# Output projection summed operand by operand, first queries asked for earlier, the gate's norm weight as a per-partition scale, and table loads moved, in a decoder block on one core

## The chip, the cores and the metric

The kernel runs on one core of a Trainium2 chip. The metric is device time in microseconds for one execution of the whole block; the median of the runs is taken. Engines are named as the profile names them: PE (TensorE, matmuls) and PEld (its weight loads), DVE (VectorE), ACT (ScalarE), POOL (GpSimd) and SP (SyncE). Here POOL and SP mainly issue transfers.

## What is computed

One decoder block over 2048 tokens of width 1024, all in float32. The input is normalised and modulated, projected once, and split between four heads of gated linear attention (GLA) and eight heads of dilated softmax attention. Their outputs are put side by side and pass through one output projection. Then follows a gated feed-forward layer with a causal convolution.

```python
h = rms_norm(x, norm1_g[l]) * (1 + sc1) + sh1
proj = h @ w_in[l]
gq, gk, gv, gr, glr, aq, ak, av = jnp.split(proj, split_at, axis=-1)
...
# gla_group, at its end
o = rms_norm(o, norm_g).reshape(B, S, H * GLA_DV)
return (o * jax.nn.silu(r.astype(jnp.float32))).astype(r.dtype)
...
mixed = jnp.concatenate([y_gla.astype(x.dtype), y_att.reshape(B, S, ATTN_DIM).astype(x.dtype)], axis=-1)
x = x + g1 * (mixed @ w_out[l])

h = rms_norm(x, norm2_g[l]) * (1 + sc2) + sh2
u = causal_depthwise_conv(h @ w_up[l], conv_w[l], conv_b[l])
u_gate, u_val = jnp.split(u, 2, axis=-1)
x = x + g2 * ((jax.nn.silu(u_gate) * u_val) @ w_down[l])
```

## The kernel before

**Tiles and products.** The sequence is cut into four chunks of T = 512 tokens. Activations lie with features on the 128 partitions, so a chunk of width 1024 is KD = 8 tiles of 128x512. Each float32 product is made of three matmuls (`mm3`, lines 317 to 319): operand and weight are each split in a high part and a remainder, and high x high, low x high, high x low are summed in a PSUM bank. For an operand the high part is a cast (ACT), the remainder a subtraction (DVE). The names are hhi and hlo, or ghi and glo, by the pool that the tiles come from; whi and wlo for weights.

**Weights.** `plan` lists the weight blocks in the order of use. `wslot` loads a block of 512 KB into one of two wraw buffers (POOL, L246), casts it to whi (ACT, L251) and subtracts for wlo (DVE, L252); whi and wlo have four buffers each. A block's request needs a free wraw buffer, and its cast a free whi buffer.

**Two streams.** Generators are woven into each other: the stream of large products (projection `proj` of all chunks, then for each chunk the output projection `outproj` and the feed-forward layer `ffn`), and beside it the mixing of each chunk, `mix(c)`: `gla` for the two halves a = 0, 1 of the chunk, then `attn` for four pairs of heads. A scheduler, given the program in this order, then orders the instructions of each engine by a timeline of its own. Each engine works its list strictly in order. The output projection of chunk 0 follows the projection of chunk 3, and runs beside the first steps of `gla(1, 0)`.

**PSUM.** Eight banks of 128x512: four (psg) for the large products, four (psa) for mixing and statistics.

**Output projection.** For each of eight column blocks cb it takes a bank and a weight block, sums over all eight operands, and adds the scaled bank to x1 (DVE, L1163). The eight operands are the mixing's outputs y, reloaded from DRAM (POOL, L1087) and split (ACT L1088, DVE L1089); the last one is still on the chip. For chunk 0 the operands are placed in pools that are free then: the first five in gp, the sixth in up, the last two in hp. The other chunks take all from hp.

**Mixing.** `gla` sums the log decays (PE L694, copied by DVE L695), forms decay factors relative to several positions (DVE L732, L735, L736 and ACT L733, L734) and multiplies them (PE L712). At its end come a Square with sums (ACT L796), a Sqrt (ACT L799), a scaling (DVE L805), transposes (PE L811), evacuations into buffers with the tag stage (two of them, shared with other users) and stores of y (SP, L814). `attn_first` loads keys kt and queries qf of a pair of heads; for later pairs it is called one pair ahead. PE L930 multiplies them. The wide projection column `wide(1)` makes the gate rg: Tanh (ACT L580), two operations of DVE (L582, and L583 with the norm weight), store.

**Norms.** For the queries and keys of attention the squares are split (ACT L520, DVE L521) and summed by PE (L526, L527); the inverse root comes from a logarithm and an exponential (ACT L528, L529), then DVE L424 to L426 and L532. The chunk's input norm does the same (PE L455, L456; ACT L461, L462), followed by DVE L479 and L483. ACT keeps one set of function tables at a time; the program holds an ACT_TABLE_LOAD wherever another is needed.

## Time and profile before

| what | us |
|---|---|
| median of 3 runs | 2571.36 |
| lowest and highest | 2571.28, 2572.19 |
| profiled execution | 2572.54 |
| its span, first to last instruction | 2570.7 |
| PE busy in it | 2536.8 (99%) |
| DVE, ACT, POOL busy | 1908.6 (74%), 1270.1 (49%), 446.9 (17%) |
| mean granted clock of PE | 0.997 of full |

Busy time is the union of an engine's instructions, so a PE that is busy may still be slow: at half clock its matmuls take longer and stay "busy". The wait of an instruction is the idle time of its engine just before it, with the instruction or transfer that ended last named behind an arrow.

### The profile page before, as it was taken

How to read it: one execution, taken by the hardware profiler on the slowest of the kernel's cores; microseconds unless marked ns; L12 is line 12 of the kernel's file. 1: busy time of each engine (PE TensorE's matmuls, PEld its weight loads, DVE VectorE, ACT ScalarE, POOL GpSimd, SP SyncE). 2: the span in 40 equal slices, each digit the busy share in tenths (PEclk: the TensorE clock that was granted, in tenths of full speed). 3: DMA queues.
4: the chain of work that ended last, by engine and by line, in shares of the span. 5: the costliest groups of instructions: out<-in, count | busy, mean ns of one | idle time of the engine just before them, and what ended most of it. 6: DMA issues, size and time to landing. Idle time of an engine off the chain costs nothing.

```text
span 2570.7 us, 49713 instructions
## 1 busy us (share of the span) xinstructions
PE 2536.8 (99%) x19458; PEld 2092.3 (81%) x19458; DVE 1908.6 (74%) x4135; ACT 1270.1 (49%) x2624; POOL 446.9 (17%) x814
## 2 busy tenths in 40 slices
PE   7999999999999999999999999999999999999999
PEld 4888788888788888888888888888888888888887
DVE  7678877767778677777977777778777776766665
ACT  5556756655554444454545444445445443433332
POOL 2333332322310000112100000310000003200001
PEclk9999999999999999999999999999999999999999
DMA  8775675665733344446434444743444536433332
GB/s 328 265 239 188 201 251 163 222 214 162 238 120 91 115 138 141 129 158 200 140 97 131 141 141 143 232 141 107 122 141 143 149 103 209 141 97 99 98 99 82
DMA packets 189727, 406.38 MB, mean 158 GB/s; under 512 B 48515, under 2 KB 89525, under 8 KB 188213
## 3 DMA queue, kind: packets, MB, share of 16 engines
q0 software_dynamic: 88096, 308.59, 36.9%
q1 hardware_dynamic: 101396, 94.60, 12.5%
q8 instruction: 154, 2.52, 0.4%
q14 instruction: 81, 0.66, 0.1%
HBM read 341.25 MB, written 61.87 MB: 157 GB/s over the span
## 4 chain that ended last, share of the span: by engine, by line
PE 93%; DVE 2%; DMA 2%; issue 1%; ACT 1%; POOL 0%; POOLq 0%; DVEq 0%; ACTq 0%
PE psg L317 27%; PE psg L318 27%; PE psg L319 27%; PE psa L907 2%; PE psa L879 2%; PE psa L1034 2%; PE psa L712 2%; PE psa L930 1%; PE psa L1028 1%; PE psa L785 0%; PE psa L784 0%; PE psa L459 0%; PE psa L789 0%; PE psg L1212 0%; DMA y<-stage 0%
## 5 line engine op out<-in xcount | busy, mean ns | idle before, releaser
L317 PE MATMUL psg<-hhi,whi 128*128 128x512 f32 x1968 | 773.0, 394 | 0.3 <-DVE x L1163 0.3
L318 PE MATMUL psg<-hlo,whi 128*128 128x512 f32 x1968 | 770.3, 392 | 0.0
L319 PE MATMUL psg<-hhi,wlo 128*128 128x512 f32 x1968 | 770.0, 391 | 0.0
L251 ACT CAST whi<-wraw 128x1024 fp32r<-128x1024 f32 (+1 forms) x388 | 407.0, 1049 | 455.6 <-PE psg L318 392.0
L252 DVE TENSOR_TENSOR wlo<-wraw,whi 128x1024 fp32r<-128x1024 f32 (+1 forms) x388 | 474.7, 1224 | 205.7 <-ACT whi L251 198.1
L317 PEld LDWEIGHTS psg<-hhi,whi 128*128 128x128 f32 x1968 | 369.9, 188 | 78.1 <-issue 0.6
L319 PEld LDWEIGHTS psg<-hhi,wlo 128*128 128x128 f32 x1968 | 369.9, 188 | 77.2 <-issue 0.3
L318 PEld LDWEIGHTS psg<-hlo,whi 128*128 128x128 f32 x1968 | 369.9, 188 | 75.9 <-issue 0.7
L317 PE MATMUL psg<-ghi,whi 128*128 128x512 f32 x744 | 296.9, 400 | 0.3 <-DVE x L1163 0.3
L318 PE MATMUL psg<-glo,whi 128*128 128x512 f32 x744 | 293.4, 394 | 1.6 <-DVE glo L1089 1.6
L319 PE MATMUL psg<-ghi,wlo 128*128 128x512 f32 x744 | 293.0, 394 | 0.0
L246 POOL DMA_DIRECT2D wraw<-in_w_up_dram x176 | 96.8, 550 | 975.8 <-DVE wlo L252 764.1
L1163 DVE SCALAR_TENSOR_TENSOR x<-psg,mod,x 128x512 f32<-128x512 f32 x192 | 143.1, 748 | 116.2 <-PE psg L319 115.8
L317 PE MATMUL psg<-whi,hhi 128*128 128x512 f32 (+2 forms) x512 | 173.8, 344 | 2.2 <-ACT stg L585 1.5
L318 PE MATMUL psg<-wlo,hhi 128*128 128x512 f32 (+2 forms) x512 | 174.4, 342 | 0.0
L319 PE MATMUL psg<-whi,hlo 128*128 128x512 f32 (+2 forms) x512 | 173.2, 341 | 0.0
L317 PEld LDWEIGHTS psg<-ghi,whi 128*128 128x128 f32 x744 | 140.5, 189 | 31.5 <-issue 0.9
L318 PEld LDWEIGHTS psg<-glo,whi 128*128 128x128 f32 x744 | 140.4, 189 | 30.7 <-DVE glo L1089 2.3
L319 PEld LDWEIGHTS psg<-ghi,wlo 128*128 128x128 f32 x744 | 140.3, 189 | 29.6 <-issue 0.2
L1118 ACT ACTIVATE y<-psg,tables_sb 128x512 f32<-128x512 f32 x176 | 135.8, 772 | 5.4 <-PE psg L319 4.8
L1119 DVE SCALAR_TENSOR_TENSOR y<-psg,tables_sb,y 128x511 f32<-128x511 f32 x176 | 130.8, 743 | 3.5 <-ACT y L1118 3.4
L1120 DVE SCALAR_TENSOR_TENSOR y<-psg,tables_sb,y 128x510 f32<-128x510 f32 x176 | 130.6, 743 | 0.5
(279 smaller groups left out, 3610.5 us busy)
## 6 DMA issues: line engine op xcount, KB each, us to landing
wraw<-in_w_up_dram POOLq DMA_DIRECT2D x176, 512.0 KB, 3.8
wraw<-in_w_down_dram POOLq DMA_DIRECT2D x88, 512.0 KB, 3.8
wraw<-in_w_ch_dram POOLq DMA_DIRECT2D x44, 512.0 KB, 4.5
wada<-in_w_ada_dram POOLq DMA_DIRECT2D x64, 256.0 KB, 4.8
wraw<-in_w_tokw_dram POOLq DMA_DIRECT2D x32, 512.0 KB, 4.6
wraw<-in_w_out_dram POOLq DMA_DIRECT2D x32, 512.0 KB, 4.5
sq<-in_xT_dram POOLq DMA_DIRECT2D x48, 256.0 KB, 5.0
x<-x POOLq DMA_DIRECT2D x48, 256.0 KB, 5.4
```

The costliest lines, as they stand in the source:

```text
L246: ld = self.dq.dma_start(raw[:, :n], src)
L251: nc.scalar.copy(hi[:, :n], raw[:, :n])
L252: nc.vector.tensor_tensor(lo[:, :n], raw[:, :n], hi[:, :n].bitcast(F32), op=ALU.subtract)
L317: nc.tensor.matmul(ps, wh, hh, start=first and k == 0, stop=False, skip_group_check=shared)
L318: nc.tensor.matmul(ps, wh, hl, start=False, stop=False, skip_group_check=shared)
L319: self.lastmm = nc.tensor.matmul(ps, wl, hh, start=False, stop=k == n - 1, skip_group_check=shared)
L712: nc.tensor.matmul(sp[j:j + w, o + n * w:o + (n + 1) * w], kh[R, k0:k0 + w], qh[R, q0:q0 + w], start=True, stop=True)
L879: nc.tensor.matmul(at(i, hh, o, n)[H[z]], q(H[hh], i, z), key(H[hh], i, k0, n), start=True, stop=True, skip_group_check=True)
L1118: nc.scalar.activation(y, ps, AF.Identity, bias=self.cb[:, b:b + 1], scale=self.cw[:, 2, b:b + 1])
L1119: nc.vector.scalar_tensor_tensor(y[:, 1:], ps[:, :T - 1], self.cw[:, 1, b:b + 1], y[:, 1:], op0=ALU.mult, op1=ALU.add)
L1120: nc.vector.scalar_tensor_tensor(y[:, 2:], ps[:, :T - 2], self.cw[:, 0, b:b + 1], y[:, 2:], op0=ALU.mult, op1=ALU.add)
L1163: nc.vector.scalar_tensor_tensor(x1, ps, self.mod[:, 40 + cb:41 + cb], x1, op0=ALU.mult, op1=ALU.add)
```

## The change

Four edits.

1. The output projection's first four blocks take four banks at once and are summed operand by operand: a new arrangement of the weights, w_outk, holds in slot j the rows of operands 2j and 2j+1 for the four blocks' 512 columns. Blocks 4 to 7 stay as they were. For chunk 0 the operands are placed anew: the first two in hp, the next five in gp, the last in up.
2. `attn_first(c, 0)` is called at the end of `gla(c, 1)`, ahead of its transposes and stores, and the queries' buffer comes from the tag pt (five buffers) instead of stage (two).
3. The gate's multiplication by the norm weight (L583) and the load of that weight are gone. The weight, a column more in the tables, times 0.5, scales the evacuation of the transposed outputs, where it is one number per partition.
4. The table set that holds logarithm and exponential is asked for after the last Tanh of `wide(1)`, and for chunk 0 after the Sqrt of `gla`, instead of at the decay's first product. The program has 29 table loads instead of 36.

```diff
@@ plan
-            yield from (("w_out", (b,), KD, P) for b in range(KD))
+            yield from (("w_outk", (j,), 2, T) for j in range(4))
+            yield from (("w_out", (b,), KD, P) for b in range(4))
@@ consts, ada_setup
-        self.gB = self.cload("gla_norm_g", (P, P))
...
+        nc.vector.tensor_scalar(self.gy, gy, 0.5, None, op0=ALU.mult)
...
+    def logexp(self, last):
+        pre = self.nc.scalar.preload_act_table_set("natural_log_exp_and_others")
+        self.tc.add_manual_dep(pre.ins, last.ins.name, mybir.DependencyInfo(mybir.DependencyClass.Sync, mybir.DependencyReason.DATA))
@@ proj, wide(1)
-                    nc.scalar.activation(st, pss[s], AF.Tanh, scale=0.5)
+                    tanh = nc.scalar.activation(st, pss[s], AF.Tanh, scale=0.5)
+                    if s == 3 and not put_off:
+                        self.logexp(tanh)
                     nc.scalar.copy(r, pss[s])
                     nc.vector.scalar_tensor_tensor(st, st, 1.0, r, op0=ALU.add, op1=ALU.mult)
-                    heads = lambda t: t.rearrange("p (a n) -> p a n", a=4)
-                    nc.vector.scalar_tensor_tensor(heads(st), heads(st), 0.5, self.gB[:, None, :].to_broadcast([P, 4, P]), op0=ALU.mult, op1=ALU.mult)
@@ the decay
-            if a == 0:
-                self.tie(nc.scalar.preload_act_table_set("natural_log_exp_and_others"), mm)
@@ gla
-        nc.scalar.activation(ss, ss, AF.Sqrt, bias=self.eps, scale=1.0 / P)
+        root = nc.scalar.activation(ss, ss, AF.Sqrt, bias=self.eps, scale=1.0 / P)
+        if c == 0:
+            self.logexp(root)
...
+        if a:
+            ready.append(self.attn_first(c, 0))
         yield
...
             st = t2("stage", 2)
-            self.copy(st, ps)
+            if s:
+                nc.scalar.activation(st, ps, AF.Copy, scale=self.gy)
+            else:
+                nc.vector.tensor_scalar(st, ps, self.gy, None, op0=ALU.mult)
@@ attn_first, attn, mix
-        qf = self.at.tile([P, T], F32, name="qf", tag="stage", bufs=2)
+        qf = self.at.tile([P, T], F32, name="qf", tag="pt", bufs=5)
...
-        kt, qf = ready.pop() if ready else self.attn_first(c, hp)
+        kt, qf = ready.pop()
@@ outproj
-            if c or k > 5:
+            if c or k < 2:
                 hi, lo = (self.hp.tile([P, T], F32R, name=n) for n in ("hhi", "hlo"))
-            elif k == 5:
+            elif k == KD - 1:
                 hi, lo = (self.up.tile([P, T], F32R, name=n, tag=n) for n in ("y0", "y1"))
...
-        for cb in range(KD):
+        def leave(cb, ps):
+            nc.vector.scalar_tensor_tensor(x1[cb], ps, self.mod[:, 16 + cb:17 + cb], x1[cb], op0=ALU.mult, op1=ALU.add)
+
+        pss = [self.pg() for _ in range(4)]
+        for j in range(4):
+            w = self.weights("w_outk", j)
+            order = [(i, cb) for i in range(2) for cb in range(4)]
+            if j == 3:
+                order.sort(key=lambda x: x[1])
+            for i, cb in order:
+                n = slice(cb * P, (cb + 1) * P)
+                self.mm3(pss[cb], [(w[i][0][:, n], w[i][1][:, n])], hs[2 * j + i:2 * j + i + 1], i == 0 and j == 0, True)
+            if j < 3:
+                yield
+        for cb in range(4):
+            leave(cb, pss[cb])
+        yield
+        for cb in range(4, KD):
             ps = self.pg()
-            self.mm3(ps, self.weights("w_out", cb), hs)
-            nc.vector.scalar_tensor_tensor(x1[cb], ps, self.mod[:, 16 + cb:17 + cb], x1[cb], op0=ALU.mult, op1=ALU.add)
+            self.mm3(ps, self.weights("w_out", cb - 4), hs)
+            leave(cb, ps)
             yield
@@ layout (host)
-        ... gla_norm_g=np.broadcast_to(gla_norm_g.reshape(1, P), (P, P)),
-        w_out=pack_blocks(w_out[0], P), ...
+        w_outk=wide(w_out[0][:, 0:512]), w_out=pack_blocks(w_out[0][:, 512:], P), ...
```

Lines below 413 keep their numbers but for one or two; later ones move on: L526 and L527 are L530 and L531 in the changed kernel, L712 is L713, L736 is L737, L796 and L799 are L797 and L800, L930 is L938, L1088 and L1089 are L1096 and L1097, L1163 of the output projection is L1102.

The scheduler's lists show the edits where they move other work. First PE, from the end of chunk 3's projection (psg_7350 is its last bank) into the output projection of chunk 0, before; psg_7495, psg_7534 and psg_7643 are the banks of blocks 0, 1 and 2, and numbers in names tell buffers apart:

```order
3010 L319 MATMUL psg_7350<-hhi_5750,wlo_7167 128x512
3011 L526 MATMUL psa_7326<-sqr_7319,blk_419 128x512
3012 L712 MATMUL psa_7377<-kt_7221 32x32 x16
3013 L712 MATMUL psa_7405<-kt_7221 32x32 x6
3014 L527 MATMUL psa_7326<-sqr_7320,blk_419 128x512
3015 L712 MATMUL psa_7405<-kt_7221 32x32 x10
3016 L712 MATMUL psa_7377<-pt_7280,pt_7279 32x32 x8
3017 L712 MATMUL psa_7405<-pt_7280,pt_7279 32x32 x8
3018 L317 MATMUL psg_7495<-ghi_7440,whi_7248 128x512
3019 L317 MATMUL psg_7534<-ghi_7440,whi_7288 128x512
3020 L317 MATMUL psg_7643<-ghi_7440,whi_7346 128x512
3021 L318 MATMUL psg_7495<-glo_7441,whi_7248 128x512
```

The same place of PE after, from the end of the projection on; psg_7484, psg_7485 and psg_7486 are blocks 0, 1 and 2, hhi_7429 and hhi_7434 the first two operands:

```order
3007 L317 MATMUL psg_7484<-hhi_7429,whi_7237 128x512
3008 L530 MATMUL psa_7315<-sqr_7308,blk_419 128x512
3009 L713 MATMUL psa_7366<-kt_7210 32x32 x16
3010 L713 MATMUL psa_7394<-kt_7210 32x32 x7
3011 L531 MATMUL psa_7315<-sqr_7309,blk_419 128x512
3012 L713 MATMUL psa_7394<-kt_7210 32x32 x9
3013 L318 MATMUL psg_7484<-hlo_7430,whi_7237 128x512
3014 L319 MATMUL psg_7484<-hhi_7429,wlo_7238 128x512
3015 L317 MATMUL psg_7485<-hhi_7429,whi_7237 128x512
3016 L318 MATMUL psg_7485<-hlo_7430,whi_7237 128x512
3017 L319 MATMUL psg_7485<-hhi_7429,wlo_7238 128x512
3018 L317 MATMUL psg_7486<-hhi_7429,whi_7237 128x512
```

The sums go on in this way to row 3029, and only then come the products that read pt (the decay factors of L736, now L737): eighteen matmuls of the output projection, one before the products with kt and seventeen behind them, now stand ahead of those.

ACT, at the norm statistics that run beside the decay factors of `gla(0, 1)`, before:

```order
242 L461 ACT_TABLE_LOAD
243 L461 ACTIVATE rstd<-psa,eps 128x512
244 L528 ACTIVATE sq<-psa,eps 128x512
245 L462 ACT_TABLE_LOAD
246 L462 ACTIVATE rstd<-rstd 128x512
247 L529 ACTIVATE sq<-sq 128x512
```

The same place after:

```order
242 L465 ACTIVATE rstd<-psa,eps 128x512
243 L532 ACTIVATE sq<-psa,eps 128x512
244 L466 ACTIVATE rstd<-rstd 128x512
245 L533 ACTIVATE sq<-sq 128x512
246 L720 COPY kt<-psa 32x128 x2
247 L522 ACTIVATE sq<-psg 128x512
```

The two loads between the statistics are gone. Ahead of it, at the end of `gla(0, 0)`, ACT after:

```order
217 L800 ACT_TABLE_LOAD
218 L800 ACTIVATE gss<-gss,eps 128x8
219 L413 ACT_TABLE_LOAD
220 L689 CAST lh<-s_2822 128x512
221 L250 CAST whi<-wraw 128x1024
```

The load of row 219, of the set with logarithm and exponential, stands right behind the Sqrt.

SP, at the end of `gla(0, 1)` and the start of the first attention, before:

```order
53 L833 DMA qn<-qn_118 128x512
54 L686 DMA rg_8468<-rg_128 128x512
55 L814 DMA y_123<-stage 128x4x128 x2
56 L825 DMA qf<-q_117 128x512 x2
57 L936 DMA v_4043<-v_122 32x2048
```

And after:

```order
52 L833 DMA qf<-q_119 128x512
53 L841 DMA qn<-qn_120 128x512
54 L687 DMA rg_8453<-rg_130 128x512
55 L833 DMA qf<-q_119 128x512
56 L822 DMA y_125<-stage 128x4x128 x2
57 L944 DMA v_4037<-v_124 32x2048
```

Both requests for queries (of the first and the second pair of heads) have come ahead of the two stores of y.

More of the change, by code (lines that the diff above doesn't have):

```diff
@@ L109 @@
 MASKS = mask_table()
-TABS = (KD, KD, 48, 1, 1, 132, 44, 4)
+TABS = (KD, KD, 48, 1, 1, 132, 44, 4, 1)
 def beside(a, na, b, nb):
@@ L328, in ada_setup @@
         o = np.cumsum((0,) + TABS)
-        self.n1, self.n2, self.ba, self.qg, self.kg, cw, self.cb, qsc = (tab[:, o[i]:o[i + 1]] for i in range(len(TABS)))
+        self.n1, self.n2, self.ba, self.qg, self.kg, cw, self.cb, qsc, gy = (tab[:, o[i]:o[i + 1]] for i in range(len(TABS)))
         self.cw = cw.rearrange("p (a b) -> p a b", a=3)
         self.qgs = self.const.tile([P, 4], F32, name="qgs")
-        self.kgs = self.const.tile([P, 1], F32, name="kgs")
+        self.kgs, self.gy = (self.const.tile([P, 1], F32, name=n) for n in ("kgs", "gy"))
         self.ones = self.const.tile([P, P], F32R, name="ones")
@@ L338, in ada_setup @@
         tanh = nc.scalar.activation(th, self.cond, AF.Tanh, scale=0.5)
-        pre = nc.scalar.preload_act_table_set("natural_log_exp_and_others")
-        self.tc.add_manual_dep(pre.ins, tanh.ins.name, mybir.DependencyInfo(mybir.DependencyClass.Sync, mybir.DependencyReason.DATA))
+        self.logexp(tanh)
         nc.vector.scalar_tensor_tensor(self.cond, th, 1.0, self.cond, op0=ALU.add, op1=ALU.mult)
@@ L578, in wide @@
                     r = stage("y1" if off else None)
-                    nc.scalar.activation(st, pss[s], AF.Tanh, scale=0.5)
+                    tanh = nc.scalar.activation(st, pss[s], AF.Tanh, scale=0.5)
+                    if s == 3 and not put_off:
+                        self.logexp(tanh)
                     nc.scalar.copy(r, pss[s])
                     nc.vector.scalar_tensor_tensor(st, st, 1.0, r, op0=ALU.add, op1=ALU.mult)
-                    heads = lambda t: t.rearrange("p (a n) -> p a n", a=4)
-                    nc.vector.scalar_tensor_tensor(heads(st), heads(st), 0.5, self.gB[:, None, :].to_broadcast([P, 4, P]), op0=ALU.mult, op1=ALU.mult)
                 else:
@@ L654, in gate @@
             for s in range(2):
-                mm = nc.tensor.matmul(ps[:, s * 256:(s + 1) * 256], glr[0:96, (2 * a + s) * P:(2 * a + s + 1) * P], self.gw, start=True, stop=True)
-            if a == 0:
-                self.tie(nc.scalar.preload_act_table_set("natural_log_exp_and_others"), mm)
+                nc.tensor.matmul(ps[:, s * 256:(s + 1) * 256], glr[0:96, (2 * a + s) * P:(2 * a + s + 1) * P], self.gw, start=True, stop=True)
             t = self.up.tile([P, T], F32, name="gt", tag="y1")
@@ L668, in gate, with gla @@
             self.tie(st, self.lastmm)
-    def gla(self, c, a):
+    def gla(self, c, a, ready):
         nc, D = self.nc, self.D[c]
@@ L1067, in mix @@
     def mix(self, c):
+        ready = []
         for a in range(2):
-            yield from self.gla(c, a)
-        ready = []
+            yield from self.gla(c, a, ready)
         for hp in range(4):
@@ L1311, in layout @@
     twice = lambda a: np.concatenate([a, a])[:, None]
-    tabs = np.concatenate([colv(norm1_g[0]), colv(norm2_g[0]), colv(b_ada[0]), twice(q_norm_g[0]), twice(k_norm_g[0]), conv_w[0].reshape(3, 44, P).transpose(2, 0, 1).reshape(P, 132), colv(conv_b[0]), scale_table()], 1).astype(np.float32)
+    tabs = np.concatenate([colv(norm1_g[0]), colv(norm2_g[0]), colv(b_ada[0]), twice(q_norm_g[0]), twice(k_norm_g[0]), conv_w[0].reshape(3, 44, P).transpose(2, 0, 1).reshape(P, 132), colv(conv_b[0]), scale_table(), colv(gla_norm_g.reshape(-1))], 1).astype(np.float32)
     arrs = dict(
@@ L1321, in layout @@
         w_ch=pack_blocks(np.concatenate([w[:, 0:512], w[:, 1552:2576]], 1), P),
-        gla_w_gate=gla_w_gate[0], gla_b_gate=gla_b_gate, gla_norm_g=np.broadcast_to(gla_norm_g.reshape(1, P), (P, P)),
-        w_out=pack_blocks(w_out[0], P), w_up=pack_blocks(w_up[0], P), w_down=pack_down(w_down[0]),
+        gla_w_gate=gla_w_gate[0], gla_b_gate=gla_b_gate,
+        w_outk=wide(w_out[0][:, 0:512]), w_out=pack_blocks(w_out[0][:, 512:], P), w_up=pack_blocks(w_up[0], P), w_down=pack_down(w_down[0]),
     )
```

## Prediction

> **What bounds the kernel.** I read the first block of the page, then the waits of TensorE, then a table of stretches around each wait, then the rows of those stretches on the engine that came last.
>
> ```profile
> span 2570.7 us, 49713 instructions
> PE 2536.8 (99%) x19458; PEld 2092.3 (81%) x19458; DVE 1908.6 (74%) x4135; ACT 1270.1 (49%) x2624; POOL 446.9 (17%) x814
> ```
>
> TensorE is busy for 99% of the span and both kernels issue the same matmuls, so an edit can only win what TensorE loses: its waits, and time at half clock. The waits, longest first:
>
> ```profile
> engine line waited for: us in total, times, longest us
> PE psa L712 <- DVE pt L736: 3.4, 1, 3.4
> PE psa L527 <- DVE sqr L521: 2.7, 1, 2.7
> PE psa L930 <- DMA qf<-q: 2.1, 1, 2.1
> PE psg L318 <- DVE glo L1089: 1.6, 1, 1.6
> PE psa L930 <- ACT stage L1057: 0.5, 1, 0.5
> ```
>
> The largest wait of that view (14.5 us, the first statistics at the start) is left out: no edit touches it. What the others cost beyond themselves is in the stretches (after PE, PEld, DVE, ACT and POOL come the granted clock, the DMA share and GB/s; the first holds the 1.5 us wait quoted further down):
>
> ```profile
> 192.00:197.00 5.00, 3.49 (x62) 2.84 (x61) 3.46 (x8) 3.99 (x8) 1.26 (x4) 1.00 0.84 309
> 295.00:300.00 5.00, 2.29 (x109) 1.51 (x110) 4.95 (x11) 4.31 (x7) 0.54 (x1) 1.00 0.20 61
> 300.00:303.50 3.50, 3.50 (x51) 2.85 (x40) 3.50 (x9) 2.48 (x4) 1.60 (x3) 0.51 0.34 112
> 375.00:378.00 3.00, 0.95 (x8) 0.72 (x6) 1.23 (x1) 1.04 (x1) 0.00 (x0) 1.00 0.68 186
> 378.00:383.00 5.00, 4.96 (x93) 4.34 (x94) 2.56 (x26) 1.69 (x4) 1.59 (x3) 0.66 0.66 195
> 657.00:666.00 9.00, 4.12 (x102) 2.62 (x101) 9.00 (x17) 7.01 (x14) 2.90 (x6) 0.77 1.08 347
> 666.00:672.00 6.00, 5.96 (x32) 4.38 (x33) 5.95 (x13) 3.81 (x12) 4.51 (x9) 0.50 0.95 318
> 672.00:680.00 8.00, 8.00 (x136) 5.83 (x135) 4.11 (x10) 1.59 (x3) 4.08 (x7) 0.99 0.88 310
> ```
>
> Each wait of 2 us or more is followed by a stretch at half clock, the one of 1.5 us by none. Lost by it: 0.49 of 3.50 us, that is 1.7, after the first; 0.34 of 5.00, that is 1.7, after the second; 0.23 of 9.00 and 0.50 of 6.00, that is 2.1 + 3.0 = 5.1, around the third. Matmuls show it directly, 0.23 us apart at full clock and 0.43 at half:
>
> ```profile
> 654.17 0.39 PE L317 MATMUL psg<-hhi,whi 128*128 128x512 f32 x1
> 654.40 0.39 PE L318 MATMUL psg<-hlo,whi 128*128 128x512 f32 x1
> ...
> 667.06 0.63 PE L317 MATMUL psg<-ghi,whi 128*128 128x512 f32 x1
> 667.49 0.63 PE L318 MATMUL psg<-glo,whi 128*128 128x512 f32 x1
> ```
>
> **Output projection of chunk 0 (657 to 672 us).** Here VectorE is busy for 9.00 of 9.00 us, and TensorE waits for it twice:
>
> ```profile
> 661.18 0.68 DVE L736 TENSOR_TENSOR pt<-kt,pt 128x512 f32<-128x512 f32 x1
> 665.31 0.68 DVE L1089 TENSOR_TENSOR glo<-glo,ghi 128x512 fp32r<-128x512 f32 x1
> ...
> 662.01 0.89 PE L712 MATMUL psa<-pt 64*32 64x32 f32 x32 [3.35 <-DVE pt L736]
> ...
> 666.04 0.80 PE L318 MATMUL psg<-glo,whi 128*128 128x512 f32 x1 [1.57 <-DVE glo L1089]
> ```
>
> The old order has nothing but the L712 products ahead of that wait. The new one has 18 output-projection matmuls there, 18 x 0.23 = 4.1 us, on operands 0 and 1, which are split first. I walked the new VectorE order with the old durations from the last row that is not held up. L736 ends near 660, the third operand's low half near 665, the next two by 666.3. TensorE, leaving the projection at 657.1, then waits about 0.6 us for the last key norm's L521, which now stands behind an operand's subtraction, and about 1.0 us for the third operand's low half. After that each operand feeds 9 to 12 matmuls, 2.0 to 2.7 us, and VectorE needs 0.6 us for one between other work. So 3.35 + 1.57 = 4.9 us of waiting become 1.6, no single one reaches 2 us, and the 5.1 us of half clock go too: 3.3 + 5.1 = -8.4. Bounds: 0 if VectorE stays the limit to the end, -10.0 if nothing waits. I take -8.4, since the matmuls put ahead (4.1 us) exceed the wait they cover (3.35).
>
> **Table loads (295 to 303).** The wait at L527 starts on ScalarE:
>
> ```profile
> 287.53 1.28 ACT L461 ACT_TABLE_LOAD   x1
> ...
> 290.11 1.28 ACT L462 ACT_TABLE_LOAD   x1
> ...
> 292.07 0.75 DVE L479 SCALAR_TENSOR_TENSOR sq<-sq,G,rstd 128x512 f32<-128x512 f32 x1 [2.32 <-ACT rstd L462]
> ...
> 298.14 0.68 DVE L521 TENSOR_TENSOR sqr<-sq,sqr 128x512 fp32r<-128x512 f32 x1
> ...
> 298.88 0.49 PE L527 MATMUL psa<-sqr,blk 128*128 128x512 f32 x1 [2.71 <-DVE sqr L521]
> ```
>
> After the first half's Sqrt the logarithm and the exponential come from separate sets, a load for each. With one load of the common set right behind the Sqrt both rows are gone: 2 x 1.28 = 2.6 us sooner on ScalarE, of which VectorE sat idle 2.32. L521 stands in the same row of work, so it ends about 2.5 to 3 us sooner; the matmul that needs it stands three matmuls (0.7 us) later in its own order. The wait of 2.71 is covered and its 1.7 us of half clock with it: -4.4, bounds 0 and -4.4. In all 7 loads of 36 go, 9 us of an engine that is 49% busy: nothing by themselves. The load added behind each Sqrt sits on ScalarE while VectorE scales the outputs; a reader of ScalarE there waits 1.28 us at worst, on no row where TensorE waits now.
>
> **First queries asked ahead (375 to 383).**
>
> ```profile
> 367.26 7.91 DMA y<-stage
> ...
> 375.19 2.72 DMA qf<-q
> ```
>
> The queries' buffer was the one from which the outputs were being stored, so their transfer began when that store landed and TensorE waited 2.1 us. Now buffer and place change: the request stands ahead of the last output stores on SP's queue, from a pool of five. Gain 2.1 + 1.7 = -3.8, and the 0.5 us of L930 on the stage in chunk 1: -4.3 together. Against it: TensorE's first use moves 39 matmuls (8.9 us) earlier, and SP's queue is in order, so a request that finds no free buffer holds the output stores behind it. The transfer of 2.7 us has more than 10 us from its new request to that use, and those stores are read by the output projection much later. Bounds: -4.3 and 0.
>
> **Gate's weight, and small things.** VectorE loses 16 operations, the projection loses one load, and each output's evacuation takes a scale, on the same engines:
>
> ```profile
> L583 DVE SCALAR_TENSOR_TENSOR stg<-stg,gla_norm_g_sb 128x512 f32<-128x512 f32 x16 | 10.9, 686 | 0.0
> ...
> 194.02 0.58 ACT L585 COPY stg<-psg 128x512 f32<-128x512 f32 x1
> ...
> 194.65 0.39 PE L317 MATMUL psg<-whi,hhi 128*128 128x272 f32 x1 [1.51 <-ACT stg L585]
> ```
>
> The 10.9 us lie beside TensorE, which nowhere waits for L583: 0. In the row of 1.51 us a bank waits for a copy that stood behind a weight cast; the new order puts two such copies ahead of it, the cast then comes last: -1.0, bounds 0 and -1.5. A column of 128 numbers scaled at the start lies in a stretch that TensorE waits for: +0.1.
>
> **The price: four banks and four weight slots at once.** For chunks 1 to 3 every operand is ready, so nothing is won; the new form must only not lose. It needs the second, third and fourth slot 1.4, 2.7 and 4.1 us after its first matmul instead of after 5.4, 10.9 and 16.3, and all four banks early:
>
> ```profile
> 1158.82 0.50 PE L317 MATMUL psg<-hhi,whi 128*128 128x512 f32 x1 [0.34 <-DVE x L1163]
> ...
> 1158.07 1.04 ACT L251 CAST whi<-wraw 128x1024 fp32r<-128x1024 f32 x1
> ...
> 1162.46 1.22 DVE L252 TENSOR_TENSOR wlo<-wraw,whi 128x1024 fp32r<-128x1024 f32 x1
> ...
> 1161.20 0.74 DVE L1163 SCALAR_TENSOR_TENSOR x<-psg,mod,x 128x512 f32<-128x512 f32 x1
> ...
> 2140.52 0.39 PE L317 MATMUL psg<-hhi,whi 128*128 128x512 f32 x1
> ...
> 2144.41 0.74 DVE L1163 SCALAR_TENSOR_TENSOR x<-psg,mod,x 128x512 f32<-128x512 f32 x1
> ```
>
> The first three rows are of chunk 1: its first matmul, the fourth slot's cast (ready 1159.1, needed at 1158.82 + 18 x 0.23 = 1162.9) and low half (ready 1163.7, first needed some 50 matmuls in, beyond 1170). So the slots cost nothing. The other rows are the drain of the last bank there and, with its first matmul, in chunk 3. Taken strictly in turn, three matmuls a bank, the fourth bank would be due nine matmuls (2.0 us) after the first: 1160.9 and 2142.6, against drained at 1161.9 and 2145.2, so 1.1 and 2.6 us late; chunk 2 is taken no worse than chunk 3. But the new order runs block 0 through six operands and block 1 after it before blocks 2 and 3 alternate, 35 matmuls or 7.9 us. Bounds 0 and 1.1 + 2.6 + 2.6 = +6.3 for the three; I take +1.0, near the end that this order shows. Last, other recurrent work stands up to 14 matmuls (3.2 us) earlier beside chunk 3's projection; bounds 0 and +3.2, I take +1.0 from waits like the 0.5 above.
>
> **Sum.** -8.4 - 4.4 - 4.3 - 1.0 + 0.1 + 1.0 + 1.0 = -16.0. The profiled execution took 2572.54 us (span 2570.7), 1.2 above the median of 2571.36; so 2556.5 for a like execution and 2555.4 for the median, -0.6%. A change under 0.2% (5.1 us) can hardly be told from none with this kernel.
>
> **A rule on the clock.** The Trainium skill (TensorE: Matmul & The Clock Gate, What's actually happening) has the clock halve after an idle window of about 3.4 us. Here 2.1 us idle were followed by half clock and 1.5 us were not, so less than a whole window was enough; if the rule held to the letter, the half-clock stretches would not be the waits' doing and would stay, and the time would be that of rival 1.
>
> **Rivals.**
> 1. Half clock stays. If those stretches (1.7 + 1.7 + 5.1 = 8.5 us) do not go with the waits, 2555.4 + 8.5 = 2563.9. For it: 2.1 us idle did what 1.5 did not, with nothing between them measured. Against: all three begin at a wait's end. 0.06.
> 2. VectorE remains the limit at the first output projection: the same additions are due in the same 9 us. If a wait of 2 us or more is left, half clock comes back; half the gain lost, 2555.4 + 4.2 = 2559.6. Against: TensorE now has other matmuls meanwhile. 0.18.
> 3. Work moved forward waits instead: the attention's first use stands 8.9 us earlier, the recurrent products 3.2. One wait of 3 us with half clock behind each of two places, 2 x (2.1 + 1.7) = 7.6: 2563.0. 0.08.
> 4. Nothing arrives, as when the removed waits reappear one instruction later: 2569 to 2571. Against: no engine but TensorE is above 74%. 0.08.
> 5. Slower: the weight slots are let go later. Block 4's cast needs the first slot, now left after some 50 matmuls instead of 24; it stands that much longer, 26 x 0.23 = 5.9 us, at the head of ScalarE's queue, with all behind it. Where TensorE needs what is behind, it waits 5.9 us less the slack, and half clock follows, 1.7 at least: up to 7.6 in each of four chunks, 30.4: 2585.8. It decides from 4.0 us a chunk (16.0 / 4). Against: behind these casts stand squares for the next norm (L440), read only after the projection, and in chunk 0 one pair of decay factors, wanted some 30 matmuls later. 0.06.
>
> **Numbers.** The forecast has the remaining 0.54. Rivals 1 to 3 are faster too, some of 3 within the bound: faster 0.82, same 0.12, slower 0.06. The low end is the sum of the best bounds: -10.0 - 4.4 - 4.3 - 1.5 = -20.2, 2551.2; the range runs to 2567, past rivals 1 to 3, which leaves out rivals 4 and 5 and a little: 0.16.
>
> **What the profile after would show.** No wait of L713 for L737 above 2 us near 660 and no half clock there; no L466 load near 290 and no wait of L531 for L525; no wait of L938 for the queries; no wait for bank drains (L1102) or for weight casts at the three later output projections; PE's busy time smaller by some 8 us. The prediction is wrong if a new wait of 2 us or more stands at any of these places, above all one at the first matmuls of blocks 1 to 3.

## The result and the profile after

The changed kernel took 2553.52 us (median of 4 runs, 2552.21 to 2560.87) against 2571.78 for the kernel before, beside it on the chip. The ratio is 0.9932 with a 95% interval of 0.9912 to 0.9953: 0.7% faster, where 0.6% was forecast. The profiled execution took 2553.83 us, 18.7 less than the one before. Three of the four runs lie within 1.6 us; the fourth, 2560.87, is 7 us above them. The first block of the profile's page:

```profile
span 2552.0 us, 49700 instructions
PE 2529.7 (99%) x19458; PEld 2087.7 (82%) x19458; DVE 1898.7 (74%) x4120; ACT 1263.2 (49%) x2617; POOL 448.2 (18%) x814
```

TensorE is busy 7.1 us less with the same matmuls, and its span is 18.7 us shorter, so 11.6 us of idle time and 7.1 us of slow matmuls are gone. The waits of TensorE after (engine, line, what it waited for: total us, times, longest):

```profile
PE psa L463 <- ACT sq L1231: 14.2, 1, 14.2
PE psg L1238 <- ACT x L496: 1.3, 2, 0.9
PE psa L531 <- DVE sqr L525: 0.9, 1, 0.9
PE psg L317 <- ACT stg L586: 0.6, 1, 0.6
PE psg L317 <- DVE x L1189: 0.3, 1, 0.3
PE psg L1238 <- ACT xg L1243: 0.2, 1, 0.2
```

Behind the start (L463, L1238) no wait reaches 1 us. The waits for L736, for the last key norm near 300, for the queries, for the operand's low half and for the copies at 194 us are gone. What took their place is 0.9 us at L531, at the very spot where the forecast set 0.6. The table of stretches after, at the same places of the program (columns as in the prediction: window, its length, busy time of PE, PEld, DVE, ACT and POOL, granted clock, DMA share, GB/s):

```profile
192.00:197.00 5.00, 5.00 (x67) 4.73 (x66) 3.82 (x8) 4.30 (x9) 4.25 (x8) 1.00 0.89 294
292.00:300.00 8.00, 8.00 (x157) 6.33 (x156) 7.95 (x18) 4.06 (x6) 2.82 (x6) 1.00 0.26 78
360.00:378.00 18.00, 18.00 (x207) 16.50 (x206) 8.51 (x43) 8.92 (x37) 5.46 (x9) 1.00 0.67 213
655.00:664.00 9.00, 9.00 (x123) 6.44 (x123) 8.94 (x20) 5.50 (x13) 4.21 (x8) 1.00 0.85 314
1140.00:1170.00 30.00, 29.66 (x207) 24.28 (x207) 21.72 (x36) 12.11 (x23) 11.47 (x21) 1.00 0.79 274
2120.00:2150.00 30.00, 30.00 (x134) 24.84 (x133) 17.40 (x24) 8.92 (x13) 11.27 (x21) 1.00 0.71 259
```

The clock is full in all six. At the first output projection (fourth row) VectorE is as busy as before, 8.94 of 9.00 us, but TensorE now works through it. The last two rows are the output projections of chunks 1 and 3: no idle time to speak of.

Both kernels issue the same number of matmuls, so the n-th large matmul of one profile can be set against the n-th of the other. How much earlier it starts, read where the two lists agree again behind each place:

| place (us of before) | gain there | gain so far | forecast there |
|---|---|---|---|
| start, to 47 | 0.3 | 0.3 | -0.1 |
| bank behind L585, 192 to 197 | 1.6 | 1.9 | 1.0 |
| table loads, 295 to 303 | 4.4 | 6.3 | 4.4 |
| first queries, 375 to 383 | 3.8 | 10.1 | 3.8 |
| between, to 653 | -0.6 | 9.5 | 0.5 - 1.0 |
| first output projection, to 690 | 8.2 | 17.7 | 8.4 |
| the rest, with the three later ones | 0.8 | 18.5 | -1.0 |

These are readings of one execution each. Two runs below (the probes of the clock) have this kernel's instructions in this order up to chunk 3's feed-forward layer. Read in the same way, the first output projection gains 6.1 and 6.3 us there, not 8.2, while the table loads and the first queries gain the same 4.4 and 3.8 to within 0.1. So differences of 2 us at the first output projection can lie between executions of one program.

### The profile page after: what moved, and what is told of

Same layout as the page of the kernel before. It is cut to its first block, busy times and chain, and to the rows that moved or that the text cites. A ratio compares the mean times of both kernels' runs of the same rounds, so it can differ in the third digit from the quotient of the medians.

```text
span 2552.0 us, 49700 instructions
## 1 busy us (share of the span) xinstructions
PE 2529.7 (99%) x19458; PEld 2087.7 (82%) x19458; DVE 1898.7 (74%) x4120; ACT 1263.2 (49%) x2617; POOL 448.2 (18%) x814
## 4 chain that ended last, share of the span: by engine, by line
PE 96%; DVE 2%; issue 1%; DMA 1%; ACT 1%; POOL 0%; SPq 0%; POOLq 0%; DVEq 0%; ACTq 0%
PE psg L317 28%; PE psg L318 27%; PE psg L319 27%; PE psa L915 2%; PE psa L887 2%; PE psa L1042 2%; PE psa L713 2%; PE psa L938 1%; PE psa L1036 1%; PE psa L786 1%; PE psa L785 1%; PE psa L463 0%; PE psa L790 0%; PE psa L531 0%; PE psg L1238 0%
## 5 line engine op out<-in xcount | busy, mean ns | idle before, releaser
L317 PE MATMUL psg<-hhi,whi 128*128 128x512 f32 x1968 | 772.3, 394 | 0.3 <-DVE x L1189 0.3
L317 PEld LDWEIGHTS psg<-hhi,whi 128*128 128x128 f32 x1968 | 369.5, 188 | 77.8 <-DVE x L1189 0.5
L317 PE MATMUL psg<-ghi,whi 128*128 128x512 f32 x744 | 295.2, 398 | 0.1
L317 PE MATMUL psg<-whi,hhi 128*128 128x512 f32 (+2 forms) x512 | 172.8, 342 | 0.6 <-ACT stg L586 0.6
L317 PEld LDWEIGHTS psg<-ghi,whi 128*128 128x128 f32 x744 | 139.6, 188 | 31.0 <-issue 0.9
```

What stands on the lines that cost most here:

```text
L317: nc.tensor.matmul(ps, wh, hh, start=first and k == 0, stop=False, skip_group_check=shared)
```

## The experiments

**Each edit alone.** Four kernels are the kernel before with one edit each, out of the diff above: the output projection's (the hunks at plan, outproj and layout, form and placement), the table loads' (the calls of logexp and the load at the decay), the first queries' (attn_first, attn, mix and the call in gla), the gate's (L583, gB, gy and the scaled evacuation).

> The kernel before with the output projection's edit alone. If each edit's gain is its own place in the trace: about 8 us less than before (the waits of 3.35 and 1.57 us at the first output projection and the half clock behind them), while the waits near 300 us (L527, 2.7) and 376 us (queries, 2.1) stay: ratio 0.997. If the gain at the first output projection needs the other edits too (VectorE freed of 16 operations, order changed by them): 0 to 4 us, with a wait over 2 us left near 660. If the three later output projections pay for the new form, waits at L1163 show there.

> The kernel before with the moved table loads alone. Own place: 4.4 us less (the wait of 2.7 at L527 and 1.7 of half clock near 300 us), all other waits as before: ratio 0.998. Rival, that the stall near 300 is VectorE's and the loads only stand beside it: wait at L527 still over 1.5 us and no change of time.

> The kernel before with the first queries asked for ahead alone. Own place: 3.8 to 4.3 us less (the wait of 2.1 and 1.7 of half clock near 376 us, and 0.5 near 511): ratio 0.998. Rival, that the request only waits for another buffer and holds the output stores behind it: a wait of similar length for the keys, the queries or a stage buffer, time unchanged or longer.

> The kernel before with the gate's norm weight as a scale alone, which leaves 16 operations of VectorE out (10.9 us). If VectorE's total load were what sets the end: several us less. If only waits of TensorE count: within 1 us of before, up to 1.6 less if the copies of L585 at 194 us come sooner by it, and the waits at 300, 376 and 660 us as before.

| edit alone | median, us | ratio to before | profiled span against before |
|---|---|---|---|
| output projection | 2565.88 | 0.9968 (0.9956 to 0.998) | -8.9 |
| table loads | 2571.17 | 0.9993 (0.9983 to 1.0002) | +0.2 |
| first queries | 2568.82 | 0.998 (0.997 to 0.9989) | -3.8 |
| gate | 2571.53 | 0.999 (0.9981 to 0.9999) | -0.1 |

The output projection's profile keeps the waits near 300 and 376 us, as expected (2.7 and 1.6 us), and the first queries gain 3.9 us at their place. The spans add up to -12.6, not to -18.7. The runs, however, show no such gap: the four ratios multiply to 0.9931, and the whole change has 0.9932, within intervals of some 2.5 us each way. The spans come from one execution each, and half clock falls differently in each. The wait for the key norm near 300 us, 2.7 us long in all five kernels without the table edit, was followed by one spell of 3.41 us at half clock in the kernel before and with the first queries alone, but by two with the output projection alone, the gate alone and the placement alone (below), which lost 1.2 to 1.4 us by it at a place that their edits don't touch. Two of them, the output projection and the placement alone, have the instructions of the kernel before in the same order up to there.

The table loads alone do what was said of their place: they bring 4.4 us there, from 1.8 us behind at 250 us to 2.6 ahead at 306. The 1.8 were lost ahead of the edit's place, 1.3 of them by 47 us, behind a wait of 1.2 us and a spell of half clock at 44 us that the kernel before doesn't show; the kernel with two edits below has the same edit and is 0.6 us ahead there. At 412 us the kernel is 0.3 us ahead. Waits of TensorE in the kernel with the table loads alone:

```profile
PE psa L934 <- DMA qf<-q: 4.5, 1, 4.5
PE psg L317 <- ACT ghi L1092: 3.1, 1, 3.1
PE psa L530 <- DVE sqr L524: 2.1, 1, 2.1
```

The wait for the queries has grown from 2.1 to 4.5 us. The output stores that hold the buffer are issued 4.0 us sooner than before (363.24 against 367.26), but TensorE reaches the place 6 us sooner (2.6 of it gained, the rest by another order of its list), and there are two spells at half clock instead of one. So 2.3 of the 4.4 us were lost here. The gate alone is a similar story: 2.0 us ahead from 208 us on, since the copies of L585 no longer wait (no line for them is left), and 0.6 ahead at 306, behind the two spells named above. Then come these waits of TensorE in the kernel with the gate's edit alone:

```profile
PE psa L931 <- DMA qf<-q: 3.9, 1, 3.9
PE psa L710 <- DVE pt L734: 3.1, 1, 3.1
```

The first has grown from 2.1 us, and by 412 us the kernel is 1.6 us behind. The second is the wait near 660, 3.4 us before: taking 10 us of work off VectorE all but leaves it. So the gain at 194 us is the gate's, and no other of its own is seen. At the queries' place, those two kernels moved as well, with nothing changed ahead of it: the output projection alone gained 1.9 us there, with a wait of 1.6 and no half clock, and the placement alone lost 0.5, with a wait of 2.5.

**Table loads and first queries together.** If the wait for the queries took up part of the tables' gain, the two edits together must show both. The kernel is the one before with these two edits, here in short:

```diff
+                    if s == 3 and not put_off:
+                        self.logexp(tanh)
...
-                self.tie(nc.scalar.preload_act_table_set("natural_log_exp_and_others"), mm)
...
+        if c == 0:
+            self.logexp(root)
...
+        if a:
+            ready.append(self.attn_first(c, 0))
...
+        qf = self.at.tile([P, T], F32, name="qf", tag="pt", bufs=5)
```

> The kernel before with the moved table loads and the earlier request together. Alone they gave +0.2 and -3.8 us in the profiled spans. If the request's wait only swallowed the tables' gain: -8.2 together (-4.4 and -3.8), no wait for queries left. If the tables' gain is lost to something else, such as VectorE at the first output projection: -4 together.

2567.21 us, ratio 0.9974 (0.9965 to 0.9984), and a profiled span 8.1 us below before, where each alone gave +0.2 and -3.8. Read by place, the tables bring 4.4 us here and the queries 3.8; no wait for queries is left. So in the profiles the earlier request keeps the tables' gain from being lost there. The runs don't show this as a gain of the pair: the two ratios alone multiply to 0.9973, against 0.9974 together, and by the medians the pair gains 6.2 us, between the two expectations.

**All but the first queries.** Taken out of the changed kernel:

```diff
-        if a:
-            ready.append(self.attn_first(c, 0))
...
-        qf = self.at.tile([P, T], F32, name="qf", tag="pt", bufs=5)
+        qf = self.at.tile([P, T], F32, name="qf", tag="stage", bufs=2)
...
-        kt, qf = ready.pop()
+        kt, qf = ready.pop() if ready else self.attn_first(c, hp)
```

> The changed kernel without the earlier request: queries in the stage buffers, asked for where the attention starts. If the gains of the edits are independent: 3.9 us slower than the changed kernel, some 2557.5. If the wait for the queries takes up what is gained ahead of it (with the table loads alone it grew from 2.1 to 4.5 us and took 5.1 us of the gain, with the gate alone 3.9 and 2.2): a wait of 4 us or more near 370 us with two windows at half clock, 8 to 11 us slower, 2562 to 2565.

2559.54 us, ratio 0.9947 (0.9929 to 0.9964); its span is 5.9 us above the changed kernel's, between the two expectations. Waits of TensorE in it:

```profile
PE psa L936 <- DMA qf<-q: 2.3, 1, 2.3
PE psa L531 <- DVE sqr L525: 2.2, 2, 1.5
```

The wait for the queries is 2.3 us, not over 4: here the scheduler placed the stores well enough, so how much this wait swallows depends on the list that comes out, not on the gain ahead of it alone. Some 3.4 us are lost there, half clock included, and 3.4 at the first output projection, where the wait at L531 has become 1.5 us and one spell of half clock follows. The second loss need not be the edit's: the probes below show a wait of 1.1 or 1.4 us and such a spell at the same place in the changed kernel's own program.

**Form or placement.** The edit of the output projection does two things for chunk 0: it changes the order of the sums, and it places the first two operands in hp. Four kernels separate them: the new form for chunk 0 alone; the new form for chunks 1 to 3 alone (chunk 0 block by block, but in the new placement); the whole change with the old placement; and the kernel before with nothing but the new placement. The first two differ from the changed kernel in which chunks take the new branch (for chunks 1 to 3, `if c:` in place of `if not c:`):

```diff
-            yield from (("w_outk", (j,), 2, T) for j in range(4))
-            yield from (("w_out", (b,), KD, P) for b in range(4))
+            if not c:
+                yield from (("w_outk", (j,), 2, T) for j in range(4))
+                yield from (("w_out", (b,), KD, P) for b in range(4, KD))
+            else:
+                yield from (("w_out", (b,), KD, P) for b in range(KD))
...
-        for cb in range(4, KD):
+        for cb in range(first, KD):
```

Here first is 4 in the new branch and 0 elsewhere. The old placement in the changed kernel is the reverse of this edit, which the last kernel makes in the kernel before:

```diff
-            if c or k > 5:
+            if c or k < 2:
...
-            elif k == 5:
+            elif k == KD - 1:
```

> The changed kernel with the operand-by-operand form for chunk 0 alone; chunks 1 to 3 take eight blocks one by one as before. If the later chunks gain nothing from the new form: the same time as the changed kernel within 1 us. If they pay for it (the forecast had +1.0, the rival of late slots or banks far more): faster than the changed kernel by that. If they gain: slower, by the 0.9 us that the aligned traces show between chunk 1 and the end.

> The changed kernel with the new form for chunks 1 to 3 alone; chunk 0 takes its blocks one by one again, but keeps the new placement of its operands (the first two in hp). If the order of the sums is what fills the wait: 7 to 9 us slower than the changed kernel, with waits of VectorE near 650 us and half clock behind them. If the placement of the operands is enough, so that the first two are split early: within 2 us of the changed kernel.

> The changed kernel with the old placement of chunk 0's operands (first five in gp, the sixth in up, the last two in hp) under the new order of sums. With the old order and the new placement the first output projection lost only 3 us of its 8. If the placement is what does it: here VectorE's wait near 650 to 660 us comes back with half clock, 6 to 9 us slower than the changed kernel, 2560 to 2563. If either of the two is enough, since any operand now feeds twelve matmuls: within 3 us of it.

> The kernel before with two lines changed: chunk 0's first two operands of the output projection lie in hp, the next five in gp, the last in up; the order of the sums stays block by block. In its instruction list twelve matmuls of the output projection stand ahead of the products with pt, where the kernel before has none and the new order under the old placement has none either. If the placement is what fills the wait: 5 to 7 us less than before, no wait of 3 us at L712 near 660 and less half clock there. If the order of the sums is needed too: under 2 us less.

| kernel | median, us | ratio to before | gain at the first output projection |
|---|---|---|---|
| changed kernel | 2553.52 | 0.9932 (0.9912 to 0.9953) | 8.2 |
| new form for chunk 0 only | 2553.63 | 0.9921 (0.9906 to 0.9936) | 8.3 |
| new form for chunks 1 to 3 only | 2555.18 | 0.9927 (0.991 to 0.9943) | 5.1 |
| old placement | 2560.41 | 0.9952 (0.9936 to 0.9968) | 1.4 |
| before, with form and placement | 2565.88 | 0.9968 (0.9956 to 0.998) | 6.9 |
| before, with placement alone | 2567.6 | 0.998 (0.9971 to 0.999) | 4.9 |

The gain is again read from the starts of matched matmuls, from 628 to 700 us of before. Placement alone brings most of it, with the old form, in both surroundings. The form alone brings 1.4. What the form adds to the new placement, 2.0 and 3.1 us, is hardly more than what executions of one program differ by (8.2 against 6.1), and by the ratios the first three rows can't be told apart. The old placement came out as expected if placement is what does it (2560 to 2563), the new form for chunks 1 to 3 only within the 2 us that were set for this; placement alone gained 3.7 us in its profiled span and 4.3 by the medians, between the 5 to 7 expected if it does everything and the 2 if the order is needed. Why is to be seen with the old placement, where the new form is there in full. The two waits of TensorE in its timeline:

```profile
649.91 0.49 PE L531 MATMUL psa<-sqr,blk 128*128 128x512 f32 x1 [1.75 <-DVE sqr L525]
652.97 1.65 PE L317 MATMUL psg<-ghi,whi 128*128 128x512 f32 x3 [1.61 <-ACT ghi L1096]
```

TensorE waits for the last key norm (L531) and then for the split of the first operand itself (L317 on ghi), so the new form had nothing ready to give it. The stretches that follow, in the same kernel, cut at the spells of the clock:

```profile
650.59:654.00 3.41, 1.80 (x35) 1.48 (x35) 3.41 (x6) 2.92 (x6) 2.32 (x5) 0.50 1.08 343
654.00:660.83 6.83, 5.85 (x75) 4.18 (x74) 6.79 (x16) 2.26 (x7) 3.00 (x6) 0.50 0.97 363
```

Half clock, 0.50, for three spells, 10.2 us. The order of the instructions agrees, and it shows the form to have no part in this. With the old placement none of the output projection's matmuls stands ahead of the products with pt, in either form. With the new placement twelve stand there in the kernel before, in the old form and in the new, and eighteen in the changed kernel, in the new form and in the old. The buffers decide: in the changed kernel's profile the two operands in hp are asked for at 635.53 us and cast from 645.6 to 646.7, while the first in gp is asked for at 647.15 us, beside the last key norm, whose squares use the same buffers, and is cast at 653.8. With placement alone the wait for VectorE at L712 near 660 is gone. The one left there is for a bank, and one spell at half clock follows it instead of three:

```profile
PE psg L317 <- ACT stg L553: 1.4, 1, 1.4
```

With the old form in the changed kernel, what is left of the waits belongs to the key norm. They stand in the timeline of the kernel with the new form for chunks 1 to 3 only:

```profile
640.65 0.50 PE L534 MATMUL psa<-sqr,blk 128*128 128x512 f32 x1 [0.66 <-DVE sqr L528]
651.10 0.51 PE L534 MATMUL psa<-sqr,blk 128*128 128x512 f32 x1 [1.54 <-DVE sqr L528]
```

And they come without half clock, as that kernel's stretch around them shows:

```profile
645.00:655.00 10.00, 8.46 (x97) 6.42 (x96) 9.54 (x14) 9.73 (x19) 4.86 (x10) 1.00 0.95 286
```

The new form for chunk 0 alone has the changed kernel's time within the spread of the runs, so chunks 1 to 3 neither pay for the new form nor gain by it that can be measured.

**What makes the clock halve.** Eleven stops in chunk 3's feed-forward layer, where TensorE has one stream only. The edit in short, without the table PROBE, which gives the number of copies, and without the ties that make the following matmuls wait for the last copy:

```diff
+                    if c == NCH - 1 and f in PROBE:
+                        for i in range(PROBE[f]):
+                            self.hold = nc.scalar.copy(self.cond[:, 0:512], self.cond[:, 512:1024])
+                            if i == 0:
+                                self.tie(self.hold, self.lastmm)
+                        self.holdn = 150
```

> The changed kernel with eleven added stops of TensorE in chunk 3's feed-forward layer, about 33 us apart: before a block all coming matmuls wait for 1 to 8 copies on ScalarE that start behind the last matmul, 0.9 to 4.6 us each. If half clock follows a wait by its length, with the border between 1.5 and 2.1 us: full clock behind the stops of 1 and 2 copies (0.9 and 1.4 us), half clock for 3.4 us or more behind those of 4, 5, 6 and 8 copies (2.4 us and longer), the stops of 3 copies in doubt. If it takes a whole idle window of 3.4 us: half clock behind 8 copies alone. If the half clock has nothing to do with the waits: none there, or some elsewhere. The place of the stop against a fixed grid of 3.41 us may decide in between: then equal stops (three of 3 copies) come out differently.

The copies are extra work, whose result nothing reads. The stops came out longer than reckoned, 3.03 us for the one copy, 2.74 for two, 0.65 more for each further one up to six, and 7.03 for eight, and half clock followed all eleven. So the lengths tell nothing, but the places do. One stop of 3.39 us, from 2254.36 to 2257.76, in the stretches of the first probe, cut along the spells of 3.413 us in which the clock changed:

```profile
2251.96:2255.37 3.41, 2.40 (x11) 1.67 (x9) 1.48 (x4) 1.83 (x3) 0.00 (x0) 1.00 0.47 154
2255.37:2258.78 3.41, 1.02 (x4) 0.86 (x5) 3.38 (x6) 2.27 (x4) 0.53 (x1) 1.00 0.23 31
2258.78:2262.20 3.42, 3.42 (x10) 2.67 (x9) 0.69 (x1) 0.62 (x1) 0.00 (x0) 0.50 0.31 125
2262.20:2265.61 3.41, 3.41 (x16) 2.82 (x15) 0.00 (x0) 0.69 (x1) 0.00 (x0) 1.00 0.00 0
```

TensorE was back at work 1.0 us before the clock fell, and the clock fell at the end of the spell, not at the end of the wait: after a spell with 1.02 us of work of 3.41, and not after the one with 2.40. The kernel with the table loads alone shows what less idle time does, each spell with the one behind it:

```profile
194.42:197.83 3.41, 1.84 (x16) 1.68 (x13) 2.36 (x7) 3.41 (x7) 1.53 (x3) 1.00 0.60 235
197.83:201.24 3.41, 3.41 (x50) 3.15 (x50) 3.41 (x6) 3.09 (x8) 2.28 (x6) 1.00 1.00 306
368.50:371.91 3.41, 1.50 (x12) 1.28 (x11) 0.76 (x2) 0.45 (x2) 1.43 (x2) 1.00 1.08 396
371.91:375.32 3.41, 0.82 (x64) 0.80 (x64) 0.00 (x0) 0.00 (x0) 0.00 (x0) 0.50 0.69 233
40.82:44.23 3.41, 2.04 (x6) 0.90 (x7) 3.41 (x8) 2.04 (x3) 0.00 (x0) 1.00 0.00 0
44.23:47.64 3.41, 3.41 (x6) 1.32 (x5) 2.92 (x4) 3.41 (x6) 2.99 (x6) 0.50 0.71 226
```

1.84 us of work kept the clock, 1.50 did not, but neither did 2.04, in the first products of the kernel. Where small products of 64x32 fill part of a spell more can be too little, as in the stretches of the kernel with the output projection's edit alone:

```profile
656.35:659.76 3.41, 2.07 (x69) 1.30 (x69) 3.41 (x6) 2.52 (x6) 1.53 (x3) 1.00 1.07 376
659.76:663.17 3.41, 3.41 (x39) 2.33 (x39) 3.41 (x6) 3.12 (x7) 1.91 (x5) 0.50 1.07 300
376.46:379.87 3.41, 2.15 (x77) 1.99 (x77) 2.20 (x17) 0.39 (x1) 0.55 (x1) 1.00 0.61 154
379.87:383.28 3.41, 3.41 (x39) 2.54 (x42) 2.82 (x12) 3.30 (x8) 1.62 (x3) 1.00 0.85 187
```

2.07 us of such mixed work, with one wait of 1.34 us, was followed by half clock; 2.15 us, with one of 1.58, was not. So between 1.84 and 2.3 us of work in a spell both outcomes are on record, and busy time alone does not draw the border.

A second probe was to make shorter stops, by tying one copy not to the last matmul but to one three to six matmuls earlier:

```diff
-                                self.tie(self.hold, self.lastmm)
+                        self.tie(self.hold, self.mms[-1 - PROBE[f]])
```

> Eleven stops of TensorE in chunk 3's feed-forward layer again, now each for one copy on ScalarE that starts 3 to 6 matmuls before the last: 1.4 to 2.1 us each by the 2.74 us of the last probe less 0.23 a matmul. In the runs so far half clock came in spells that begin on a grid of 3.413 us, behind a spell with 1.91 us or more of idle, and not behind one with 1.57. If the idle share of one spell of that grid decides: half clock only behind spells with more than 1.6 to 1.9 us idle, equal stops differ by where they fall, and a stop that a border cuts in halves costs nothing more. If the length of the wait decides: all stops of one length come out alike.

It made none. The 1.4 to 2.1 us that were expected took the 2.74 us of two copies for one. A copy that starts three to six matmuls early was done before TensorE ran out of work, and the feed-forward layer shows neither a wait above 0.8 us nor half clock. So it says only that the half clock of the first probe was the stops' doing. A dense series of stops across the border is left open.

This run shows something else. Up to chunk 3's feed-forward layer its engines work the same instructions in the same order as in the changed kernel, and yet half clock is back at the first output projection. Its wait for the last key norm, and the stretches there:

```profile
PE psa L540 <- DVE sqr L534: 1.1, 1, 1.1
```

```profile
647.32:650.73 3.41, 2.29 (x70) 1.56 (x69) 3.41 (x7) 3.20 (x6) 2.85 (x6) 1.00 1.11 329
650.73:654.14 3.41, 3.41 (x10) 2.62 (x9) 3.41 (x6) 3.06 (x7) 1.71 (x4) 0.50 1.01 377
```

The first probe has a wait of 1.4 us and one spell at half clock there too. With 0.9 us in the changed kernel's profile, and 0.7 with the new form for chunk 0 only, there was none.

## Why the prediction was right, and where not

- **Output projection of chunk 0: -8.4, measured -8.2.** The wait left at L531 was set at 0.6 us and measured 0.9; the second one, 1.0 us for the third operand's low half, did not come. The half clock went in this execution, but one spell of it, 1.7 us, came back in the two probes behind waits of 1.1 and 1.4 us, so the hit to 0.2 us is in part luck. What failed is the reason given: the prediction credits "the new order" of the sums for the matmuls ahead of the wait. The instruction lists and the runs show that the placement of the first two operands puts them there, in either order. Placement alone gave 4.9 us, the order alone 1.4, both 6.9 on the kernel before.
- **Table loads: -4.4, measured -4.4** at their place, in the changed kernel and in all kernels with this edit. TensorE's chain through L465, L466 and VectorE is shorter by the two loads. The traces show 38 table loads before and 31 after: seven fewer, as said, though not 36 and 29. The prediction counted it as a gain by itself. Alone its runs gave a ratio of 0.9993 (0.9983 to 1.0002), 1.8 us, at most 4.4; in its profile (+0.2) 2.3 us were lost at the queries, and the rest elsewhere.
- **First queries: -3.8, measured -3.8**, here and in every kernel with this edit. Without it the changed kernel's span is 5.9 us longer, of which 3.4 lie at this place. The 0.5 us on the stage in chunk 1 went too, but 0.6 was lost between 383 and 653 us; the prediction had set +1.0 for work moved forward against it.
- **Gate: "0" for the 16 operations, -1.0 for the copies at 194 us.** The two are one: with the gate's edit alone the wait at L585 goes, without it 1.1 to 1.6 us of it stay. Measured -1.6, so the second term was too small. Which part of the edit lets the copies come sooner is not separated; if it is the 16 operations, their 0 was wrong.
- **Banks and slots at chunks 1 to 3: +1.0, measured none.** The new form for chunk 0 alone is no faster. The lower bound was the right end.
- **The rivals.** Half clock did not stay (1): it is nowhere at these places in the profile after, though one spell came back in the two probes. VectorE stayed as busy (2), but not the limit. Work moved forward (3) cost 0.6 us, not 7.6, and no removed wait came back one instruction later (4). The later casts (5) held up nothing that TensorE wanted.
- **The clock.** The Trainium skill's rule of an idle window (TensorE: Matmul & The Clock Gate, What's actually happening) is not borne out to the letter: 1.9 us idle of a spell of 3.41 was enough. The prediction's own reading, a wait of 2 us or more, holds for the waits that it was read from, but not for others (1.1, 1.3 and 1.4 us at the first output projection): what counts is what TensorE does in one spell, and so where in the grid a wait falls. That no wait of 2 us was left was therefore not enough to say that half clock would go.

## What to carry to other kernels

When an engine waits at a seam between two stages, look first at which buffers hold the next stage's first operands: two of them in a pool that was already free were worth more here than a new order of the sums. A gain ahead of a transfer that starts on its own chain can be lost in the wait for it, so look for the gain behind that wait too. Read a place in more than one execution, and hold sums of profiled spans against the runs: single edits gave 12.6 us by their spans, all together 18.7, and yet the ratios of the runs multiply to just what the whole change has. And count a stall of TensorE with what the clock adds: in the kernel before five spells at half clock cost 8.5 us beside 9.8 us of waits.

## What was not expected of the hardware

The half clock comes in spells of 3.413 us that begin on a fixed grid: in the first probe the starts 2204.17, 2231.48, 2258.78 and 2286.09 lie 27.30 or 27.31 us apart, eight spells, although the stops ahead of them began at other distances (26.54, 26.42, 27.07). Between 30 and 2500 us of the fourteen profiles every spell at full clock with 1.76 us of work or less was followed by one at half clock, and none with more than 2.3. A wait of 1.5 us cost only itself at 194 us in the kernel before, since the grid cut it in two, while one of 1.3 us at 658 us, within one spell, cost 1.7 more in the kernel with the output projection's edit alone. The two spells of the first:

```profile
190.80:194.21 3.41, 2.34 (x40) 1.64 (x39) 1.87 (x6) 1.20 (x2) 0.54 (x1) 1.00 1.00 378
194.21:197.63 3.42, 2.98 (x32) 2.79 (x33) 3.42 (x8) 3.42 (x8) 1.73 (x4) 1.00 0.72 262
```

Half clock mostly ended behind a spell in which TensorE worked through, but not always. In the kernel with the output projection's edit alone, behind the wait of 2.7 us, a spell full of mostly small products was followed by another at half clock:

```profile
297.95:301.36 3.41, 3.41 (x107) 2.84 (x107) 3.41 (x7) 3.05 (x4) 1.06 (x2) 0.50 0.16 46
301.36:304.78 3.42, 3.42 (x9) 2.65 (x9) 3.42 (x8) 0.92 (x2) 0.53 (x1) 0.50 0.83 278
```

The same wait was followed by one spell at half clock in the kernel before, so equal waits of one program need not cost the same. Second, a table load on ScalarE cost its 1.28 us in the rows and hardly more: it began 0.02 us after the end of the operation ahead of it (287.11 + 0.40, then 287.53), and the operation behind it began 0.01 us after it (287.53 + 1.28, then 288.82).
